# Where matmul operands start: ring tiles 64 bytes longer, 512-column operands level with the large buffers, values operands 64 bytes above

## The chip, the core and the metric

The kernel runs on one core of a Trainium2 chip. The metric is the device time of one execution in microseconds; lower is better. Before the change it is 1809.54 us, the median of 3 runs (1808.73 to 1810.48).

## What is computed

Two inputs, a prompt and a sample, each of 512 tokens by 1024, pass through the same two layers in fp32: one of differential attention, one of bidirectional retention. The reference, cut to what matters:

```python
def trunk(x, ...):
    for i in range(2):
        h = rms_norm(x, norm_g[i], 1e-6)
        x = x + (diff_attention(h, ...) if i == 0 else bidir_retention(h, ...))
    return rms_norm(x, final_norm_g, 1e-6)

def diff_attention(h, w_in, ...):
    q, k, v, gate = split(h @ w_in)            # 1024 -> 4 * 2048, 8 heads
    p = softmax(q @ k.T)                       # two score maps a head, rotary q and k
    a = p[:, :, 0] - lam * p[:, :, 1]
    o = rms_norm(a @ v, subln_g) * silu(gate)
    return o @ w_out                           # 2048 -> 1024
```

`bidir_retention` has the same frame (projection, gate, output projection); its scores are masked by a decay instead of a softmax, forward and backward, and carry a state from one half of the sequence to the other.

## The kernel before

**Three passes for a product.** An fp32 operand is split into a high part of reduced precision (fp32r) and the rest. A product takes three matmuls (`PASSES`, line 32): high by high, high by low, low by high. The high part is cast by ScalarE (`hi_of`, line 399, recorded at line 400), the rest is a subtraction on VectorE (`lo_of`, line 402, recorded at line 403).

**Projections.** The input projections are made in 2 by 2 blocks with seven products P1 to P7 for eight (`SEQ`, line 43). `make_b` (line 448) makes the seven transposed activation operands B11 to T4, each of four tiles of 128 by 2 by 512, in 28 large buffers ("slots"). A `Unit` (line 518) is 512 columns of weights. `prep` (line 551) puts a weight operand in a tile of the ring `ws` (7 tiles of 4096 bytes a partition), and `product` (line 586) multiplies:
- a "pair" unit (q, k and gate) streams the large buffer, 512 columns, past weights from the ring: line 599;
- a "wide" unit (values) streams the ring tile, 256 columns, past weights from the large buffer: line 609.

**Attention and retention.** Scores of the first layer stream k past q, 512 columns (line 1116); the product of the score map with the values is at line 1181, 256 columns. Its transposes are at line 1161. In the second layer, lines 1315 (scores), 1339 (state), 1359 and 1367 (output) all have 256 columns. The output projection of either layer streams a ring tile of `out_weights` (line 862), 512 columns, past the head's output oT (line 891).

**Where buffers lie.** 18 of the large buffers are cuts of one tile, the arena, 4096 bytes apart (`slot`, line 303); the others (numbers 12, 13 and from 20 on) are tiles of the pool `cp`. A cut may be shifted by some elements of 4 bytes: k of the first layer by 16, v by 16, oT by 32 (`new_oT`, line 826), and so on. A shifted cut reaches into the next one's start, so each has a second name, its edge, by which the planner sees such neighbours. The arena begins with 32 unused elements and is 80 longer than its 18 cuts. Small columns (row maxima, sums, scales, a few elements each) have a pool `sm` of their own, which lies first; the ring is in the pool `wk` with the other work tiles, behind the arena.

**Who sets the order.** Every operation is recorded with a cost, what it reads and what it writes. `Plan.arrange` (line 138) simulates the engines with these costs and writes an order for each engine by hand; matmuls keep the recorded order within a window of 24. The order therefore depends on the names by which operations are tied, edges among them, and not on addresses. Loads go through SyncE's queue.

Of the kernel before, what the change touches and what calls it, by code (L numbers as in the profile page):

```python
# [9 lines left out]
F32 = mybir.dt.float32  # L10
F32R = mybir.dt.float32r
# [4 lines left out]
P = 128  # L16
S = 512
D = 1024
KT = D // P
NT = S // P  # L20
NH = 8
# [11 lines left out]
WS_BUFS = 7  # L33
# [220 lines left out]
def trunk_kernel(  # L254
# [9 lines left out]
    ys = (y_prompt, y_sample)  # L264
    plan = Plan()

    sm = ctx.enter_context(tc.tile_pool(name="sm", bufs=1))
    cp = ctx.enter_context(tc.tile_pool(name="cp", bufs=1))
    ar = ctx.enter_context(tc.tile_pool(name="ar", bufs=1))
    wk = ctx.enter_context(tc.tile_pool(name="wk", bufs=1))  # L270
# [2 lines left out]
    dr = ctx.enter_context(tc.tile_pool(name="dr", bufs=1, space=bass.MemoryType.DRAM))  # L273


    SIZE = dict(ws=1024, raw=1024, st=1024, c=512, e=512, m=512, os=1024)
    places = {}
    cnt = [0]

    def view(pool, tag, i, size, shape, dt=F32):  # L280


        if size % 16 and pool in (cp, wk):
            pool = sm
        if (tag, i) not in places:
            places[tag, i] = pool.tile([P, size], F32, tag=f"{tag}{i}", name=f"{tag}_{i}", bufs=1)
        n = math.prod(shape[1:])
        t = places[tag, i][0:shape[0], 0:n]
        if dt != F32:
            t = t.bitcast(dt)  # L290
        if len(shape) == 3:
            t = t.rearrange("p (a b) -> p a b", a=shape[1])
        elif len(shape) == 4:
            t = t.rearrange("p (a b c) -> p a b c", a=shape[1], b=shape[2])
        return t

    def work(tag, shape, bufs, dt=F32, name=None):
        size = SIZE.get(tag, shape[1])
        return Buf(plan, tag, bufs, lambda i: view(wk, tag, i, size, shape, dt))

    arena = ar.tile([P, 18 * 1024 + 80], F32R, tag="arena", name="arena")

    def slot(n, shape, dt=F32R, shift=0):

        size = math.prod(shape[1:])
        at = None if n in (12, 13) or n >= 20 else n if n < 12 else n - 2
        if at is None:
            assert not shift  # L310
            cnt[0] += 1
            label = f"b_{cnt[0]}"
            return Buf(plan, f"b{n}", 1, lambda i: cp.tile(shape, dt, tag=f"b{n}", name=label))
        assert dt == F32R
        lo = 32 + at * 1024 + shift

        def make(i):
            t = arena[:, lo:lo + size]
            return t.rearrange("p (a b) -> p a b", a=shape[1]) if len(shape) == 3 else t
        b = Buf(plan, f"b{n}", 1, make)  # L320
        b.also = Buf(plan, f"edge{at + 1 if shift else at}", 1, None)
        return b

    def const(shape, tag, dt=F32, size=None):
        return Buf(plan, tag, 1, lambda i: view(cp, tag, i, size or math.prod(shape[1:]), shape, dt))

    def ws_t(shape):
        return work("ws", shape, WS_BUFS, F32R)

    def raw_t(shape):  # L330
        return work("raw", shape, 4)
# [1 line left out]
    def st_t(shape, name="st"):  # L333
        return work("st", shape, 3, name=name)
# [18 lines left out]
    def bank(tag, name=None):  # L353
        return Buf(plan, tag, BUFS[tag], lambda i: view(pj if tag == "pj" else sc, tag, i, S, [P, S]))
# [16 lines left out]
    def dve(n, fn, r, w, wait=0.0):  # L371
        plan.op("DVE", 0.07 + 0.00104 * n, fn, r, w, wait=wait)
# [20 lines left out]
    def dma(out, in_, r, w, kb, eng=None):  # L393

        q = eng or nc.sync
        plan.op("SP" if eng is None else "ACT", 0.62, lambda: q.dma_start(out(), in_()), r, w, lands=2.0 + kb / 200.0,
                kb=kb, load=any(isinstance(k[0] if isinstance(k, tuple) else k, Buf) for k in w))

    def hi_of(n, dst, src, r, w):
        act(n, lambda: nc.scalar.copy(dst(), src()), r, w)  # L400

    def lo_of(n, dst, src, hi, r, w):
        dve(n, lambda: nc.vector.tensor_tensor(dst(), src(), hi().bitcast(F32), op=ALU.subtract), r, w)  # L403
# [39 lines left out]


    Bop = {}
    powers = const([P, NH, NT], "powers", size=64)

    def make_b(layer, source):


        def parts(name, k, hi, lo, r):
            t = slot(B_SLOT[name] + k, [P, 2, S])
            hi(lambda: t[:, 0, :], r, [(t, 0)])
            lo(lambda: t[:, 1, :], lambda: t[:, 0, :], r + [(t, 0)], [(t, 1)])
            Bop[name, k] = t
# [62 lines left out]
    class Unit:  # L518
# [32 lines left out]
        def prep(self, op):  # L551
            x = self.take
            n = 256 if self.wide else P

            def combine(a, b, fn):
                t = st_t([P, 4, n])
                out = ((lambda: self.like(t.t)), t)
                dve(4 * n, lambda: nc.vector.tensor_tensor(out[0](), a[0](), b[0](), op=fn), [a[1], b[1]], [t])
                return out
            if op == "P1":  # L560
                src = x(0, 0)
            elif op == "P2":
                src = x(0, 1)
            elif op == "P4":
                src = x(1, 1)
            elif op == "P5":
                src = self.s[1] = combine(x(1, 0), x(1, 1), ALU.add)
            elif op == "P6":
                src = self.s[2] = combine(self.s[1], x(0, 0), ALU.subtract)
            elif op == "P3":  # L570
                src = combine(x(0, 1), self.s[2], ALU.subtract)
            else:
                src = combine(x(0, 0), x(1, 0), ALU.subtract)
            if self.wide:
                a, b = ws_t([P, 4, n]), ws_t([P, 4, n])
                hi, lo = ((lambda: a.t), a), ((lambda: b.t), b)
            else:
                s = ws_t([P, 2, 4, n])
                hi, lo = ((lambda: s[:, 0]), (s, 0)), ((lambda: s[:, 1]), (s, 1))
            hi_of(4 * n, lambda: self.like(hi[0]()), src[0], [src[1]], [hi[1]])  # L580
            lo_of(4 * n, lambda: self.like(lo[0]()), src[0], lambda: self.like(hi[0]()), [src[1], hi[1]], [lo[1]])
            self.ops[op] = (hi, lo)
            if op == "P2" and self.early is not None:
                self.early, self.x = None, {}
# [239 lines left out]
        return rr  # L824

    def new_oT(g):
        return [slot(16 + 2 * g + a, [P, 2, S], F32R, 32) for a in range(2)]

    def load_qk(src, i, shift):
        t = slot(i, [P, 2, S], F32R, shift)  # L830
        dma(lambda: t.t.bitcast(F32), lambda: src[0][src[1]], [src[0]], [t], 512)
        return t
# [95 lines left out]
    qk_d = {}  # L928
# [164 lines left out]
    qk, vt, sg, oT = {}, {}, {}, {}  # L1093
    st = [{} for _ in tiles]

    def fetch1(h, g, v=True):
        for j in range(2):
            for which in range(2):
                qk[h, g, j, which] = load_qk((qk_d[0, which, h, g], j), 6 * which + 2 * g + j, 16 * which)
        if v:  # L1100
            fetch1_v(h, g)

    def fetch1_v(h, g):
        vt[h, g] = load_v(v_d[0, h, g], 10 + 4 * g, 16)
        sg[h, g] = load_sg(g_d[0, h, g])
# [108 lines left out]
    def at(f, i, n):  # L1214
        if 0 <= i < n:
            f(i)

    fetch1(0, 0)
    fetch1(0, 1, False)
    turns2 = itertools.chain(["sc", "o", "sc", "o"], itertools.cycle(["tp", "o"]))  # L1220
    made = make_b(1, x_source(1, xN, lambda g: next(turns2) if g else "pj"))

    for i in range(N + 5):
        if i % 2 and i > 2:
            fill(1, LAG)
            at(av, i - 3, N)
        at(scores, i, N)
        at(row_max, i, N)
        at(exps, i, N)
        at(combine, i, N)  # L1230
        for n, when in enumerate((0, 1, 2, 3)):
            if i == when:
                step(proj, 1)
                if n >= 2:
                    new_xN(n - 2, lambda t, n=n: (xs[n - 2][0, t * P:(t + 1) * P, :], []))
                if n == 3:
                    fetch1_v(0, 1)
        if not i % 2 or i < 3:
            fill(1, LAG)
        at(transp, i - 1, N)  # L1240
        fill(1, LAG)
        if i % 2 == 0 and i > 3:
            at(weighed, i - 4, N)
        if i < N and i % 4 == 2 and i > 4:
            nh, ng = tiles[i][0:2]
            if ng == 1 and nh + 1 < NH:
                fetch1(nh + 1, 0)
            elif ng == 0 and nh > 0:
                fetch1(nh, 1)
# [20 lines left out]
    qk, vt, sg, oT = {}, {}, {}, {}  # L1270
# [78 lines left out]
    def av2(b, c):  # L1349
# [29 lines left out]
        if c == 0:  # L1379
            settle(h - 1, g)  # L1380
            oT[h, g] = new_oT(g)
# [71 lines left out]
    for i in range(N2 + 1):  # L1453
        if i < N2:
            b, c = chunks[i]
# [8 lines left out]
            if i == N2 - 1:  # L1464
                for n in range(2):
                    f = fin_ps[n] = bank("sc", "fin")
# [67 lines left out]
```

## Time and profile before

| | |
|---|---|
| median of 3 runs | 1809.54 us |
| span of the profiled execution | 1807.0 us |
| TensorE busy | 1794.9 us, 10299 matmuls |
| weight loads (PEld) | 1558.1 us |
| VectorE, ScalarE, GpSimd busy | 1477.1, 895.1, 169.5 us |
| mean granted TensorE clock | 0.999 |
| DMA | 328.81 MB, 182 GB/s on average |

The span runs from the first to the last instruction of one profiled execution, and its sums are compared with that span; the runs' time is some 2.5 us above it. In lines of the timeline, the first two numbers are the start in us and the duration of a merged row of like instructions; a matmul's end is modelled and overlaps the next one's start, so the pace is the distance from one row's start to the next row's. In grouped lines, the pair behind the bar is busy time in us and mean ns of one instruction, followed by the engine's idle time before them. In the chain, the pair is the start and the duration of a piece.

### The profile page before, as it was taken

The numbers are of one execution on the slowest core, as the hardware profiler recorded it, in microseconds if no ns is written. First come the engines' busy times: TensorE is split into PE (matmuls) and PEld (weight loads), VectorE is DVE, ScalarE is ACT, GpSimd is POOL, SyncE is SP. The second block draws the span as 40 slices with busy tenths as digits, with TensorE's granted clock in tenths as the row PEclk, the third lists the DMA queues.
The fourth block names the chain that finished last, engine by engine and source line by source line (L and its number), as shares of the span: only waits on it lengthen the run. The fifth ranks groups of instructions, "written<-read, shape, count | busy, mean of one in ns | idle before, by whom it ended". The sixth has DMA issues, their size and how long they took to land.

```text
span 1807.0 us, 27780 instructions
## 1 busy us (share of the span) xinstructions
PE 1794.9 (99%) x10299; PEld 1558.1 (86%) x10299; DVE 1477.1 (82%) x2319; ACT 895.1 (50%) x1856; POOL 169.5 (9%) x323
## 2 busy tenths in 40 slices
PE   9999999999999999999999999999999999999998
PEld 6789889898988888888888888898989898888887
DVE  7958787778699888888888897787887967888887
ACT  7753444433434565554555866444434355444346
POOL 1000000000000022222322300000000000111113
PEclk9999999999999999999999999999999999999999
DMA  6444455555545685444554524464657559765662
GB/s 217 134 126 137 161 140 178 184 168 155 174 126 175 201 334 198 178 156 159 190 204 140 190 73 146 140 210 146 205 156 228 151 170 396 272 238 182 225 218 94
DMA packets 162767, 328.81 MB, mean 182 GB/s; under 512 B 12724, under 2 KB 76872, under 8 KB 162632
## 3 DMA queue, kind: packets, MB, share of 16 engines
q1 hardware_dynamic: 162304, 326.71, 54.1%
q8 instruction: 81, 1.33, 0.3%
q14 instruction: 54, 0.44, 0.1%
q10 hardware_dynamic: 328, 0.34, 0.1%
HBM read 209.55 MB, written 117.44 MB: 181 GB/s over the span
## 4 chain that ended last, share of the span: by engine, by line
PE 93%; DVE 2%; DMA 2%; ACT 2%; issue 1%; POOL 0%; SPq 0%; POOLq 0%; DVEq 0%; ACTq 0%
PE pj L599 20%; PE pj L891 19%; PE sc L599 10%; PE pj L609 10%; PE o L599 8%; PE o L1181 5%; PE sc L1116 5%; PE sc L609 5%; PE o L609 2%; PE o L1359 2%; PE tp L1161 2%; PE sc L1315 1%; PE o L1367 1%; PE tp L1339 1%; DMA raw<-in_ret_w_out_dram 1%
## 5 line engine op out<-in xcount | busy, mean ns | idle before, releaser
L891 PE MATMUL pj<-ws,arena 128*128 128x512 f32 x1542 | 391.2, 397 | 0.0
L891 PEld LDWEIGHTS pj<-ws,arena 128*128 128x128 f32 x1542 | 277.7, 188 | 52.7
L599 PE MATMUL pj<-b,ws 128*128 128x512 f32 x1080 | 265.0, 392 | 0.0
L599 PEld LDWEIGHTS pj<-b,ws 128*128 128x128 f32 x1080 | 201.4, 188 | 43.0
L403 DVE TENSOR_TENSOR ws<-st,ws 128x512 fp32r<-128x512 f32 (+1 forms) x192 | 147.9, 774 | 74.8 <-ACT ws L400 56.7
L896 DVE SCALAR_TENSOR_TENSOR b<-pj,crr,b 128x512 f32<-128x512 f32 (+1 forms) x257 | 189.9, 744 | 21.4 <-PE pj L891 21.0
L403 DVE TENSOR_TENSOR ws<-raw,ws 128x512 fp32r<-128x512 f32 (+1 forms) x164 | 141.5, 868 | 71.3 <-ACT ws L400 61.0
L400 ACT CAST ws<-st 128x512 fp32r<-128x512 f32 (+1 forms) x192 | 132.4, 693 | 121.4 <-PE pj L599 36.4
L599 PE MATMUL sc<-arena,ws 128*128 128x512 f32 x768 | 186.8, 392 | 0.0
L599 PE MATMUL o<-arena,ws 128*128 128x512 f32 x744 | 180.0, 393 | 1.1 <-ACT m L385 0.6
L599 PEld LDWEIGHTS sc<-arena,ws 128*128 128x128 f32 x768 | 144.0, 188 | 31.3
L400 ACT CAST ws<-raw 128x512 fp32r<-128x512 f32 (+1 forms) x164 | 125.7, 772 | 87.0 <-PE o L599 45.0
L599 PEld LDWEIGHTS o<-arena,ws 128*128 128x128 f32 x744 | 138.4, 188 | 31.7 <-DVE arena L463 1.4
L599 PE MATMUL pj<-arena,ws 128*128 128x512 f32 x648 | 160.3, 392 | 0.4 <-DVE arena L463 0.4
L599 PEld LDWEIGHTS pj<-arena,ws 128*128 128x128 f32 x648 | 120.8, 188 | 26.7 <-DVE arena L463 0.7
L1134 ACT ACTIVATE b<-sc,nm 128x512 f32<-128x512 f32 x128 | 88.0, 689 | 66.9 <-DVE nm L1124 66.5
L636 ACT COPY c<-pj 128x512 f32<-128x512 f32 x104 | 60.9, 586 | 119.7 <-PE pj L599 66.4
L609 PE MATMUL pj<-ws,b 128*128 128x256 f32 x960 | 116.8, 276 | 0.0
L609 PEld LDWEIGHTS pj<-ws,b 128*128 128x128 f32 x960 | 113.2, 188 | 0.7
L1116 PE MATMUL sc<-arena 128*128 128x512 f32 x384 | 101.2, 395 | 0.3 <-ACT b L1134 0.3
L1181 PEld LDWEIGHTS o<-arena 128*128 128x128 f32 x768 | 93.1, 188 | 2.7
L1181 PE MATMUL o<-arena 128*128 128x256 f32 x768 | 93.7, 278 | 0.0
(207 smaller groups left out, 2855.9 us busy)
## 6 DMA issues: line engine op xcount, KB each, us to landing
qk<-os SPq DMA_DIRECT2D x192, 256.0 KB, 3.6
arena<-qk SPq DMA_DIRECT2D x96, 512.0 KB, 5.8
raw<-in_da_w_in_dram SPq DMA_DIRECT2D x64, 512.0 KB, 5.1
v<-os SPq DMA_DIRECT2D x64, 512.0 KB, 4.3
arena<-v SPq DMA_DIRECT2D x64, 512.0 KB, 4.1
raw<-in_ret_w_in_dram SPq DMA_DIRECT2D x48, 512.0 KB, 4.8
os<-g SPq DMA_DIRECT2D x32, 512.0 KB, 7.4
g<-e SPq DMA_DIRECT2D x48, 256.0 KB, 4.6
```

Source lines behind the costliest of these rows:

```text
L400: act(n, lambda: nc.scalar.copy(dst(), src()), r, w)
L403: dve(n, lambda: nc.vector.tensor_tensor(dst(), src(), hi().bitcast(F32), op=ALU.subtract), r, w)
L599: nc.tensor.matmul(ps.t, a[u][0]()[:, k, :], bt[k][:, v, :], start=(opens and k == 0 and i == 0), stop=(k == 3 and i == 2), skip_group_che ...
L609: nc.tensor.matmul(ps[:, (t % 2) * 256:(t % 2) * 256 + 256], bt[k][:, v, t * P:(t + 1) * P], a[u][0]()[:, k, :], start=(opens and t % 2 == ...
L636: act(S, lambda c=c, ps=ps: nc.scalar.copy(c.t, ps.t), [ps], [c])
L891: nc.tensor.matmul(ps[:, here], o[a][:, e, t * P:(t + 1) * P], u[b][:, e, here], start=(m == 0), stop=(m == 5))
L896: axpy(n, lambda half=half, here=here, ps=ps: nc.vector.scalar_tensor_tensor(half, ps[:, here], rr[:, t % 2:t % 2 + 1], half, op0=ALU.mult ...
L1116: nc.tensor.matmul(s.t, q[:, a, t * P:(t + 1) * P], k[:, b, :], start=(n == 0), stop=(n == 2))
L1134: act(840, lambda j=j, s=s, m=m: nc.scalar.activation(p[:, j, :], s.t, AF.Exp, bias=m.t, accum_out=sm[:, 2 * j + n:2 * j + n + 1]), [s, m] ...
L1161: nc.tensor.transpose(tp[:, j * P:(j + 1) * P], p[:, 0, j * P:(j + 1) * P], ident.t)
L1181: nc.tensor.matmul(o[:, e * 256:(e + 1) * 256], v[b][:, j, e * P:(e + 1) * P], aT[a][:, j, :], start=(n == 0), stop=(n % 12 == 11), skip_g ...
L1359: nc.tensor.matmul(o[:, e * 256:(e + 1) * 256], v_[v][:, 2 * c + j, e * P:(e + 1) * P], a_[:, u, j * 256:(j + 1) * 256], start=(e == 0 and ...
```

## The change

The pool of small columns goes. Each of the 7 ring tiles becomes 1024 + 16 elements, a tile of its own in the arena's pool, directly behind the arena. Between two ring tiles lies a pad of 48 elements, and columns of up to 32 elements are cut from these pads one after another. A ring tile is used from its start by 512-column matmuls (pair units, output projection), and from element 16 on, 64 bytes above, by values products (`wide`). The arena loses its 32 leading elements; k of the first layer loses its shift; oT's shift grows from 32 to 64 elements.

With this, the large buffers in `cp`, the arena's unshifted cuts and the ring tiles all start at the same place modulo 256 bytes, and oT too, whose shift is 256 bytes.

```diff
-    sm = ctx.enter_context(tc.tile_pool(name="sm", bufs=1))
...
     def view(pool, tag, i, size, shape, dt=F32):
-        if size % 16 and pool in (cp, wk):
-            pool = sm
+        n = math.prod(shape[1:])
         if (tag, i) not in places:
-            places[tag, i] = pool.tile([P, size], F32, tag=f"{tag}{i}", name=f"{tag}_{i}", bufs=1)
-        n = math.prod(shape[1:])
+            if size <= 32 and pool in (cp, wk):
+                k = next(k for k, used in enumerate(gaps) if used + size <= PAD - 16)
+                places[tag, i] = pads[k][:, gaps[k]:gaps[k] + size]
+                gaps[k] += size
+            else:
+                places[tag, i] = pool.tile([P, size], F32, tag=f"{tag}{i}", name=f"{tag}_{i}", bufs=1)
...
-    arena = ar.tile([P, 18 * 1024 + 80], F32R, tag="arena", name="arena")
+    PAD = 64
+    gaps = [0] * (WS_BUFS - 1)
+    arena = ar.tile([P, 18 * 1024 + 64], F32R, tag="arena", name="arena")
+    rings, pads = [], []
+    for i in range(WS_BUFS):
+        rings.append(ar.tile([P, 1024 + 16], F32R, tag=f"ws{i}", name=f"ws_{i}"))
+        if i < WS_BUFS - 1:
+            pads.append(ar.tile([P, PAD - 16], F32, tag=f"pad{i}", name=f"pad_{i}"))
...
-        lo = 32 + at * 1024 + shift
+        lo = at * 1024 + shift
...
-    def ws_t(shape):
-        return work("ws", shape, WS_BUFS, F32R)
+    def ws_t(shape, wide=False):
+        def make(i):
+            lo = 16 if wide else 0
+            t = rings[i][:, lo:lo + 1024]
+            if len(shape) == 3:
+                return t.rearrange("p (a b) -> p a b", a=shape[1])
+            return t.rearrange("p (a b c) -> p a b c", a=shape[1], b=shape[2])
+        return Buf(plan, "ws", WS_BUFS, make)
...
-    powers = const([P, NH, NT], "powers", size=64)
+    powers = const([P, NH, NT], "powers")
...
-                a, b = ws_t([P, 4, n]), ws_t([P, 4, n])
+                a, b = ws_t([P, 4, n], True), ws_t([P, 4, n], True)
...
-        return [slot(16 + 2 * g + a, [P, 2, S], F32R, 32) for a in range(2)]
+        return [slot(16 + 2 * g + a, [P, 2, S], F32R, 64) for a in range(2)]
...
-                qk[h, g, j, which] = load_qk((qk_d[0, which, h, g], j), 6 * which + 2 * g + j, 16 * which)
+                qk[h, g, j, which] = load_qk((qk_d[0, which, h, g], j), 6 * which + 2 * g + j, 0)
```

More of the change, by code (lines that the diff above doesn't have):

```diff
@@ L273, in trunk_kernel @@
     dr = ctx.enter_context(tc.tile_pool(name="dr", bufs=1, space=bass.MemoryType.DRAM))
-    SIZE = dict(ws=1024, raw=1024, st=1024, c=512, e=512, m=512, os=1024)
+    SIZE = dict(raw=1024, st=1024, c=512, e=512, m=512, os=1024)
     places = {}
```

## The prediction

> **What bounds the kernel now.** I read the core's span and clock first, then the busy line of the page, then the chain of waits, then PE's waits.
>
> ```profile
> core 0: 1807.0 us, clock 0.999
> PE 1794.9 (99%) x10299; PEld 1558.1 (86%) x10299; DVE 1477.1 (82%) x2319; ACT 895.1 (50%) x1856; POOL 169.5 (9%) x323
> PE 93%; DVE 2%; DMA 2%; ACT 2%; issue 1%; POOL 0%; SPq 0%; POOLq 0%; DVEq 0%; ACTq 0%
> PE sc L1010 <- DVE minus L411: 1.4, 1, 1.4
> PE tp L1028 <- DVE arena L463: 1.0, 2, 0.7
> ```
>
> TensorE has work for 1794.9 of 1807.0 us at a clock of 0.999, the chain is 93% PE, and the two longest of PE's waits are 1.4 and 1.0 us in total. So the end is set by how fast matmuls follow each other. The "mean ns of one" of a matmul (about 392) overlaps its neighbours; the pace has to be read from starts. The longest pieces of the chain are the cleanest place, since the same instruction repeats there without a wait:
>
> ```profile
> 75.27 8.24 PE pj L599 x36
> 1783.58 13.76 PE pj L891 x60
> ```
>
> 36 matmuls of 512 columns in 8.24 us are 228.9 ns each; 60 of the output projection in 13.76 us are 229.3. The pace of 256 columns comes from the timeline, as the distance between the starts of two rows:
>
> ```profile
> 303.18 5.60 PE L609 MATMUL sc<-ws,arena 128*128 128x256 f32 x48
> 308.62 0.84 PE L609 MATMUL pj<-ws,b 128*128 128x256 f32 x6
> ```
>
> 308.62 - 303.18 = 5.44 us over 48 is 113.3 ns. Two of them take 226.7: a 512-column matmul costs 2.2 ns more than its two halves would. Remember this number; it is the term that the forecast uses.
>
> **What the change moves.** No operation is added or removed; every engine has as many instructions as before. What moves is where operands lie. From the placement in the built programs, each operand's start modulo 256 bytes, moving minus stationary:
> - L599 (moving: large buffer; stationary: ring tile), L891 (ring; oT) and L1116 (k; q): +64 before, 0 after.
> - L609 (moving: ring tile; stationary: large buffer): -64 before, +64 after.
> - L1181, L1339, L1315 (-64) and L1359, L1367 (+64): unchanged.
> Also, large buffers and rings began 32 bytes beyond a multiple of 64; now they begin on a multiple of 64.
>
> How many matmuls this touches:
>
> ```profile
> L891 PE MATMUL pj<-ws,arena 128*128 128x512 f32 x1530 | 389.8, 398 | 0.0
> L599 PE MATMUL pj<-b,ws 128*128 128x512 f32 x1080 | 265.0, 392 | 0.0
> L599 PE MATMUL sc<-arena,ws 128*128 128x512 f32 x768 | 186.8, 392 | 0.0
> L599 PE MATMUL o<-arena,ws 128*128 128x512 f32 x744 | 180.0, 393 | 1.1 <-ACT m L385 0.6 <-DVE arena L463 0.3
> L599 PE MATMUL pj<-arena,ws 128*128 128x512 f32 x648 | 160.3, 392 | 0.4 <-DVE arena L463 0.4
> L599 PE MATMUL sc<-b,ws 128*128 128x512 f32 x120 | 29.1, 391 | 0.0
> L1116 PE MATMUL sc<-arena 128*128 128x512 f32 x384 | 101.2, 395 | 0.3 <-ACT b L1134 0.3
> L609 PE MATMUL pj<-ws,b 128*128 128x256 f32 x960 | 116.8, 276 | 0.0
> L609 PE MATMUL sc<-ws,arena 128*128 128x256 f32 x768 | 89.6, 276 | 0.0
> L609 PE MATMUL pj<-ws,arena 128*128 128x256 f32 x576 | 73.1, 277 | 0.0
> L609 PE MATMUL o<-ws,arena 128*128 128x256 f32 x384 | 45.0, 277 | 0.0
> ```
>
> 512 columns: 1530 + 3360 (the five L599 rows) + 384 = 5274. Values products: 960 + 768 + 576 + 384 = 2688.
>
> **(1) 512 columns, +64 to 0.** No steady run of the profile has level operands, so the price is bounded by the nearest rows. First, does an offset matter at all? One stretch of the second layer holds runs at both offsets:
>
> ```profile
> 1603.61 0.86 PE L1339 MATMUL tp<-arena 128*128 128x256 f32 x6
> 1604.31 0.87 PE L1315 MATMUL sc<-arena 128*128 128x256 f32 x6
> 1605.01 1.54 PE L891 MATMUL pj<-ws,arena 128*128 128x512 f32 x6
> 1606.39 1.52 PE L1359 MATMUL o<-arena 128*128 128x256 f32 x12
> 1607.75 0.84 PE L1367 MATMUL o<-arena,b 128*128 128x256 f32 x6
> 1608.43 1.55 PE L891 MATMUL pj<-ws,arena 128*128 128x512 f32 x6
> ```
>
> Distances of starts: L1359 (+64) 1.36/12 = 113.3 and L1367 (+64) 0.68/6 = 113.3, but L1339 and L1315 (-64) 0.70/6 = 116.7. The six L891 take 1.38 us; five at 228.9 leave 235.5 for the sixth, during which the weights of L1359 are read, 64 bytes above the ring tile that streams. So about 3.4 ns per 256 columns and 6.6 per 512 can hang on where operands lie. But -64 isn't always dear: L609 (-64) runs at 113.3. Two places show a level weight read once, at the end of a run:
>
> ```profile
> 1303.79 2.91 PE L599 MATMUL pj<-arena,ws 128*128 128x512 f32 x12
> 1306.54 5.63 PE L609 MATMUL pj<-ws,b 128*128 128x256 f32 x48
> 926.12 2.90 PE L1181 MATMUL o<-arena 128*128 128x256 f32 x24
> 928.86 1.54 PE L1116 MATMUL sc<-arena 128*128 128x512 f32 x6
> ```
>
> The twelfth L599 streams a large buffer while L609's weights, from another large buffer, are read: both start 32 bytes past a multiple of 256. Twelve take 2.75 us, 229.2 each: a single level read costs nothing that shows. L1181's last one is level with L1116's weights too: 24 take 2.74 us, 114.2 each, near the pace of 113.3.
> Bounds per 512-column matmul, then: dearest +6.6 ns (the sixth L891): 5274 x 6.6 = +34.8 us. Cheapest, without another mechanism: as fast as its two halves, 228.9 - 226.7 = -2.2 ns: -11.6 us. I take -2.2. The surplus of 2.2 over two halves exists only at 512 columns, the level read seen once isn't dear, and operand offset is the one thing that differs for it; the rows at -64 are an offset that the 512s never have, before or after. The choice is an inference; the trace has no steady level run that proves it.
>
> **(2) Values products, -64 to +64.** 113.3 before (L609) and 113.3 for the rows that already have +64 (L1359, L1367): 0. If they fell to the pace of L1315 instead, 2688 x 3.4 = +9.1 us.
>
> **(3) Small columns between the ring tiles.** Their writers and readers keep their order in kind; they are ACT, DVE and POOL work that is hidden behind PE: ACT has half of the span free, POOL 91%, and DVE 18%. Waits stay nearly as many in the built program (PE: 1114 on other engines' semaphores and DMAs before, 1109 after), so sharing a tile adds no chain of false waits: 0. If DVE's free 330 us (1807.0 - 1477.1) were eaten, DVE would be the bound; that needs each of its 2319 instructions to grow by 142 ns.
>
> **(4) Order.** q and k tiles without a shift touch other neighbours in the arena, and the planner's order changes in one place: PE's order is the same up to matmul 3394 and differs for some 250 of the next 300, where attention begins. That is inside this window:
>
> ```profile
> 620.00:690.00 70.00, 69.69 (x387) 59.04 (x387) 54.95 (x92) 42.45 (x103) 12.45 (x30) 1.00 0.88 325
> ```
>
> Columns after the stretch are PE, PEld, DVE, ACT and POOL busy, clock, DMA share, GB/s. PE idles 0.3 of 70 us, with the DMA at 0.88. Moving a few products by one place can win at most 0.3 us, and lose about what PE's two longest waits above cost, 1 to 2 us, if a product comes ahead of its load. I take 0, bounds -0.3 and +2.
>
> **Sum.** -11.6 + 0 + 0 + 0: 1807.0 - 11.6 = 1795.4 us for the profiled execution. The median of the runs is 1809.5, 2.5 above that span, so 1797.9 on the metric.
>
> **Rivals.**
> - *Level weight reads disturb the stream* (slower). In a long level run every weight load, not one, meets the moving reads, and each matmul pays what L1315 pays over L1359, 3.4 ns, up to the 6.6 of the sixth L891. For it: those rows. Against: the two level places above. 5274 x 3.4 = +17.9 us: 1827.4; at 6.6, 1844.3. It decides as soon as 36 chained L599 take longer than 8.24 us, and shows on the whole kernel from +0.7 ns each.
> - *Offsets don't matter for 512 columns* (the change does nothing to time). For it: 229.2 with a level read against 228.9 without; L609 at -64 as fast as L1359 at +64. Then 1809.5.
>  The Trainium skill, SBUF — State Buffer, section "SBUF: two separate sides", has PE on ports of its own that never wait on anyone, and TensorE: Matmul & The Clock Gate, section "Part 2: What happens when you issue a matmul", gives it two independent read ports, one for the moving operand and one for LDWEIGHTS. By that rule this rival is right. L609 agrees with it (113.3 at -64); L1315's 116.7 against L1359's 113.3, same size, doesn't.
> - *The start on a multiple of 64 is what helps* (much faster). A 512-column operand that begins 32 bytes off a multiple of 64 touches 33 pieces of 64 bytes, an aligned one 32. If each piece costs the same, a matmul saves 228.9/33 = 6.9 ns: 5274 x 6.9 = 36.4 us, 1773.1; with the 2688 values products saving 113.3/17 = 6.7 as well, another 18 us: 1755. For it: 113.3 is 17 times 6.67. Against: 228.9 isn't 33 times 6.67 (220), and nothing in this trace starts aligned.
>  The Trainium skill, TensorE: Matmul & The Clock Gate, section "Back-to-back issue gap", has 512 columns at N/2.4 + 2.5 = 215.8 ns; an estimate by it would be 5274 x 13.1 = 69 us off. No run here shows that pace.
>
> **How the numbers follow.** About 0.2% (3.6 us) is what a measurement of this kernel can tell from no change. Forecast, -2.2 ns per 512 columns: 0.42. Aligned starts, or another gain that is larger: 0.13. Nothing: 0.12. Level reads disturb: 0.28. The rest slower (values products at L1315's pace, or the shared tile of small columns delaying DVE): 0.05. Faster is thus 0.55, same 0.12, slower 0.33. The range goes from the 512-column saving of aligned starts (1773, taken as 1772) to between the slower rival's two prices (1827 and 1844), 1838. The forecast's own range, if its mechanism holds, is 1793 to 1806.
>
> **What would show it.** Right: chain pieces of 36 L599 at about 8.16 us (36 x 226.7) and L891 alike, L609 still 48 in 5.44, span near 1795. Wrong, slower: L599 pieces over 8.24 with L609 unchanged. Aligned starts: 36 L599 near 7.99 us, and L609 at 48 in 5.12; L1359 and L1367, whose offset isn't changed, also faster, which only this rival expects. Nothing: all pieces as quoted. If (2) is wrong, L609 alone moves; if (3), PE shows new waits for DVE, ACT or POOL; if (4), idle of PE in 620 to 690.

## The result and the profile after

The change makes the kernel slower: 1817.93 us, the median of 5 runs (1817.51 to 1818.54), against 1809.54 (5 runs, 1808.50 to 1810.48). The ratio is 1.0044, with a 95% interval of 1.0032 to 1.0057. The profiled execution has a span of 1815.6 us, 8.6 above that of before. Line numbers have moved by 17: L616 is what was L599, L626 was L609, L908 was L891, L1133 was L1116, L1198 was L1181, and L1332, L1356, L1376 and L1384 were L1315, L1339, L1359 and L1367. Below, the lines are called by the work that they do, with the number of before.

Three lines of the page of after, the span, the busy line and the chain's shares, answer to those of before:

```profile
core 0: 1815.6 us, clock 0.999
PE 1801.2 (99%) x10299; PEld 1572.6 (87%) x10299; DVE 1477.2 (81%) x2319; ACT 895.1 (49%) x1856; POOL 171.6 (9%) x323
PE 92%; DMA 3%; DVE 2%; ACT 1%; issue 0%; SPq 0%; POOL 0%; POOLq 0%; DVEq 0%; ACTq 0%
```

The clock is the same, VectorE, ScalarE and GpSimd are within 2.1 us of their old sums, and PE still carries the chain. PE's busy time grew by 6.3 us and its idle time by 2.3 (1815.6 - 1801.2 = 14.4 us against 12.1). So the loss is mostly in the pace of matmuls. From the chain of after, start and duration of two of its longest pieces:

```profile
1149.55 8.16 PE pj L616 x36
1792.27 13.66 PE pj L908 x60
```

These are faster: 36 in 8.16 us are 226.7 ns each instead of 228.9, just what was forecast, and the output projection's 60 take 227.7 instead of 229.3. The values products, from the timeline of after:

```profile
303.06 5.81 PE L626 MATMUL sc<-ws,arena 128*128 128x256 f32 x48
308.71 0.87 PE L626 MATMUL pj<-ws,b 128*128 128x256 f32 x6
```

48 of them take 308.71 - 303.06 = 5.65 us instead of 5.44: 117.7 ns each instead of 113.3. The second layer's stretch, again from the timeline of after:

```profile
1610.97 0.88 PE L1356 MATMUL tp<-arena 128*128 128x256 f32 x6
1611.68 0.85 PE L1332 MATMUL sc<-arena 128*128 128x256 f32 x6
1612.37 1.55 PE L908 MATMUL pj<-ws,arena 128*128 128x512 f32 x6
1613.76 1.58 PE L1376 MATMUL o<-arena 128*128 128x256 f32 x12
1615.17 0.87 PE L1384 MATMUL o<-arena,b 128*128 128x256 f32 x6
1615.88 1.55 PE L908 MATMUL pj<-ws,arena 128*128 128x512 f32 x6
```

L1376's twelve now take 1.41 us, where the same twelve took 1.36; L1384's six take 0.71 instead of 0.68. Neither line's operands were moved against each other by the change. And the six of the output projection take 1.39 us, as long as before (1.38). Over the whole trace its 129 runs of six gained nothing (237.7 ns each on average, 237.6 before), while its 53 runs of twelve went from 234.5 to 231.9 ns each and the long run at the end gained too.

With all starts of each trace added up, line by line (from each start to the next, in us):

| line of before | before | after | difference |
|---|---|---|---|
| L599, projections, 512 | 774.3 | 768.5 | -5.8 |
| L891, output projection, 512 | 360.8 | 359.1 | -1.7 |
| L1116, scores, 512 | 89.8 | 90.5 | +0.7 |
| L609, values products, 256 | 305.7 | 317.1 | +11.4 |
| L1181, map by values, 256 | 88.4 | 90.0 | +1.6 |
| L1359 and L1367, output of layer two, 256 | 65.9 | 68.3 | +2.4 |
| L1315 and L1339, 256 | 45.1 | 45.1 | 0 |

These rows make +8.6 us, the difference of the spans; smaller rows, which are left out, cancel to within 0.4. The 512s gain 6.8 us, the 256s lose 15.4. The +0.7 of L1116 is no slower pace: its row holds one wait, for ScalarE's work at L1134 (L1151 in the kernel after), in which two starts lie 1.35 us apart.

### The profile page after: what moved, and what is told of

The parts are those of the page before. It is cut to its first block, busy times and chain, and to the rows that moved or that the text cites. A ratio compares the mean times of both kernels' runs of the same rounds, so it can differ in the third digit from the quotient of the medians.

```text
span 1815.6 us, 27774 instructions
## 1 busy us (share of the span) xinstructions
PE 1801.2 (99%) x10299; PEld 1572.6 (87%) x10299; DVE 1477.2 (81%) x2319; ACT 895.1 (49%) x1856; POOL 171.6 (9%) x323
## 4 chain that ended last, share of the span: by engine, by line
PE 92%; DMA 3%; DVE 2%; ACT 1%; issue 0%; SPq 0%; POOL 0%; POOLq 0%; DVEq 0%; ACTq 0%
PE pj L616 20%; PE pj L908 19%; PE sc L616 10%; PE pj L626 10%; PE o L616 8%; PE sc L626 5%; PE o L1198 5%; PE sc L1133 4%; PE o L626 2%; PE o L1376 2%; PE tp L1178 1%; PE o L1384 1%; PE tp L1356 1%; PE sc L1332 1%; DMA raw<-in_ret_w_out_dram 1%; DVE ws L420 1%
## 5 line engine op out<-in xcount | busy, mean ns | idle before, releaser
L908 PE MATMUL pj<-ws,arena 128*128 128x512 f32 x1542 | 389.6, 396 | 0.0
L908 PEld LDWEIGHTS pj<-ws,arena 128*128 128x128 f32 x1542 | 277.6, 188 | 50.7
L616 PE MATMUL pj<-b,ws 128*128 128x512 f32 x1080 | 263.1, 391 | 0.2 <-DVE e L661 0.2
L616 PEld LDWEIGHTS pj<-b,ws 128*128 128x128 f32 x1080 | 201.4, 188 | 41.7 <-DVE e L661 0.6
L913 DVE SCALAR_TENSOR_TENSOR b<-pj,pad,b 128x512 f32<-128x512 f32 (+1 forms) x257 | 190.5, 745 | 22.0 <-PE pj L908 21.2
L616 PE MATMUL sc<-arena,ws 128*128 128x512 f32 x768 | 185.2, 390 | 0.0
L616 PE MATMUL o<-arena,ws 128*128 128x512 f32 x744 | 178.8, 391 | 1.1 <-ACT m L402 0.6
L616 PEld LDWEIGHTS sc<-arena,ws 128*128 128x128 f32 x768 | 144.0, 188 | 29.8
L616 PEld LDWEIGHTS o<-arena,ws 128*128 128x128 f32 x744 | 138.4, 188 | 30.6 <-DVE arena L480 1.4
L616 PE MATMUL pj<-arena,ws 128*128 128x512 f32 x648 | 159.2, 391 | 0.3 <-DVE arena L480 0.3
L616 PEld LDWEIGHTS pj<-arena,ws 128*128 128x128 f32 x648 | 120.9, 188 | 25.6 <-DVE arena L480 0.6
L1151 ACT ACTIVATE b<-sc,pad 128x512 f32<-128x512 f32 x128 | 87.9, 688 | 69.8 <-DVE pad L1141 68.9
L626 PE MATMUL pj<-ws,b 128*128 128x256 f32 x960 | 120.8, 280 | 0.0
L626 PEld LDWEIGHTS pj<-ws,b 128*128 128x128 f32 x960 | 117.0, 188 | 0.6
L1133 PE MATMUL sc<-arena 128*128 128x512 f32 x384 | 99.9, 394 | 0.9 <-ACT b L1151 0.9
L1198 PEld LDWEIGHTS o<-arena 128*128 128x128 f32 x768 | 94.4, 189 | 3.2 <-ACT arena L417 0.7
L1198 PE MATMUL o<-arena 128*128 128x256 f32 x768 | 95.2, 281 | 0.5 <-ACT arena L417 0.5
```

Of the source, the lines that this page charges most:

```text
L616: nc.tensor.matmul(ps.t, a[u][0]()[:, k, :], bt[k][:, v, :], start=(opens and k == 0 and i == 0), stop=(k == 3 and i == 2), skip_group_che ...
L626: nc.tensor.matmul(ps[:, (t % 2) * 256:(t % 2) * 256 + 256], bt[k][:, v, t * P:(t + 1) * P], a[u][0]()[:, k, :], start=(opens and t % 2 == ...
L908: nc.tensor.matmul(ps[:, here], o[a][:, e, t * P:(t + 1) * P], u[b][:, e, here], start=(m == 0), stop=(m == 5))
L913: axpy(n, lambda half=half, here=here, ps=ps: nc.vector.scalar_tensor_tensor(half, ps[:, here], rr[:, t % 2:t % 2 + 1], half, op0=ALU.mult ...
L1133: nc.tensor.matmul(s.t, q[:, a, t * P:(t + 1) * P], k[:, b, :], start=(n == 0), stop=(n == 2))
L1151: act(840, lambda j=j, s=s, m=m: nc.scalar.activation(p[:, j, :], s.t, AF.Exp, bias=m.t, accum_out=sm[:, 2 * j + n:2 * j + n + 1]), [s, m] ...
```

## The experiments

Two questions: is it the new offset of the values products that costs (their own +64 bytes), or something that follows from the level 512s; and what of the 512s' gain holds alone. Offsets are, as in the prediction, moving operand minus stationary operand, modulo 256 bytes. The table gives the pace of each kind in ns, from start to start inside the runs of a line, over the whole trace of each kernel, and the ratio to the kernel before on the same chip. Where runs are short (L891, L1181, L1359), such a mean moves by up to half a ns with the distances that are left out of it. Matmuls come in the order of before in e3, e5, e6 and e13, and in the order of the change in the others; the two orders differ only where attention begins.

| kernel | median us | ratio, 95% | L599 | L891 | L609 | L1181 | L1359 |
|---|---|---|---|---|---|---|---|
| before | 1809.54 | | 228.9 | 229.4 | 113.3 | 114.6 | 113.8 |
| after | 1817.93 | 1.0044, 1.0032 to 1.0057 | 226.9 | 227.5 | 117.8 | 116.9 | 117.5 |
| e1, values at 0 | 1823.44 | 1.0075, 1.0060 to 1.0090 | 226.8 | 228.8 | 120.0 | 117.0 | 117.4 |
| e2, all 32 bytes on | 1817.51 | 1.0044, 1.0029 to 1.0059 | 226.9 | 228.8 | 117.8 | 116.8 | 117.4 |
| e3, before, starts on 64 | 1809.79 | 1.0001, 0.9992 to 1.0011 | 228.9 | 229.4 | 113.4 | 114.6 | 113.3 |
| e4, values at -64 | 1816.67 | 1.0041, 1.0026 to 1.0055 | 226.8 | 227.9 | 117.5 | 117.7 | 117.4 |
| e5, old offsets, new layout | 1809.03 | 1.0003, 0.9994 to 1.0013 | 228.9 | 229.3 | 113.4 | 115.6 | 113.3 |
| e6, only L599 level | 1813.28 | 1.0027, 1.0016 to 1.0038 | 226.8 | 229.2 | 117.5 | 115.4 | 113.4 |
| e7, only L891 and L1116 level | 1811.61 | 1.0019, 1.0009 to 1.0028 | 228.9 | 227.9 | 113.4 | 117.7 | 117.4 |
| e8, values at +32 | 1813.37 | 1.0028, 1.0016 to 1.0040 | 226.8 | 227.4 | 116.7 | 117.0 | 117.4 |
| e13, only values at +64 | 1821.99 | 1.0072, 1.0058 to 1.0085 | 228.9 | 229.3 | 117.8 | 115.6 | 113.9 |

### First round: which offset costs

**e1: values products level too**, the change with

```diff
-            lo = 16 if wide else 0
+            lo = 0
```

> The changed kernel with the values operands level too (0 instead of +64). Its profile showed 512-column matmuls at 226.8 ns (228.9 before) but values products at 117.8 (113.3 before). Theory 'start' (the place of an operand relative to a multiple of 64 bytes sets the pace of 256 columns: 113.3 at 32 past, 117.8 on it): L609 stays at 117.8, about 1818 us. Theory 'offset' (moving minus stationary sets it; +64 is worse than -64): L609 leaves 117.8, either way. Theory 'rhythm' (256 columns keep the rhythm in which the 512-column runs leave the array, and level runs leave a worse one): 117.8, 1818.

Measured: 1823.44 us. In its timeline, where the change has 5.65:

```profile
303.80 5.92 PE L626 MATMUL sc<-ws,arena 128*128 128x256 f32 x48
309.56 0.88 PE L626 MATMUL pj<-ws,b 128*128 128x256 f32 x6
```

48 in 5.76 us: 120.0 ns. Level is the worst of the places tried for values products, and the best one found for 512 columns. So an offset isn't good or bad as such.

**e2: the change, 32 bytes on**, so that all large operands start 32 bytes beyond a multiple of 64, as before the change, with the offsets between them kept:

```diff
+    lead = cp.tile([P, 8], F32, tag="lead", name="lead")
```

> The changed kernel with one unused tile of 32 bytes in front, so that every large buffer and ring tile starts 32 bytes past a multiple of 64, as before the change; all offsets between operands stay those of the change. Theory 'start': L609 back to 113.3 (2688 x 4.4 ns = 11.9 us off) and L1181, L1359, L1367 back too (some 3 us), 512 columns stay at 226.8: 1802 to 1806 us. Theories 'offset' and 'rhythm': as the changed kernel, 1818.

Measured: 1817.51 us, and L599 and the values products at the pace of the change; only L891 is some 1 ns slower than there, as it is in e1, with the same offsets. **e3: the kernel before, on a multiple of 64**, its old offsets kept:

```diff
-    gcol = const([P, 28], "gcol")
+    gcol = const([P, 24], "gcol")
```

> The kernel before with one column tile 16 bytes shorter, which moves all large buffers and ring tiles 32 bytes down, onto multiples of 64; offsets between operands stay those of before. Theory 'start': L609 at 117.8 and the other 256-column lines up too, 512 columns unchanged at 228.9: about 1822 to 1825 us. Theories 'offset' and 'rhythm': as before, 1809.5.

Measured: 1809.79 us, a ratio of 1.0001. Where operands start in absolute terms, on a multiple of 64 or 32 beyond it, does nothing to the time that can be measured in either kernel. What counts is how far apart the two operands of a matmul are.

**e4: 512s level, values products back at -64**, by a ring that begins 64 bytes lower:

```diff
-    arena = ar.tile([P, 18 * 1024 + 64], F32R, tag="arena", name="arena")
+    arena = ar.tile([P, 18 * 1024 + 112], F32R, tag="arena", name="arena")
...
-            lo = 16 if wide else 0
+            lo = 0 if wide else 16
```

> The changed kernel with ring tiles 64 bytes lower relative to the large buffers and the two uses swapped: 512 columns from element 16 (level, as in the change), values products from element 0 (-64, as before the change). Theory 'offset': L609 back to 113.3, about 1806 us. Theories 'start' and 'rhythm': L609 at 117.8, 1818.

Measured: 1816.67 us; values products at 117.5 ns although their offset is the old one, at which the kernel before has 113.3. Undoing the edit that the loss sits on doesn't undo the loss. Something else in the change slows them too.

### Second round: one part at a time

**e5: the new layout with all old offsets** (the pool of small columns gone, columns in the pads, the ring behind the arena):

```diff
-    arena = ar.tile([P, 18 * 1024 + 64], F32R, tag="arena", name="arena")
+    arena = ar.tile([P, 18 * 1024 + 112], F32R, tag="arena", name="arena")
...
-                a, b = ws_t([P, 4, n], True), ws_t([P, 4, n], True)
+                a, b = ws_t([P, 4, n]), ws_t([P, 4, n])
...
-        return [slot(16 + 2 * g + a, [P, 2, S], F32R, 64) for a in range(2)]
+        return [slot(16 + 2 * g + a, [P, 2, S], F32R, 32) for a in range(2)]
...
-                qk[h, g, j, which] = load_qk((qk_d[0, which, h, g], j), 6 * which + 2 * g + j, 0)
+                qk[h, g, j, which] = load_qk((qk_d[0, which, h, g], j), 6 * which + 2 * g + j, 16 * which)
```

> Control: pads, packed columns, ring stride and order of the change, but every offset between operands as before it (512 columns +64, values -64, k shifted by 16, oT by 32). If the offsets alone carry the loss (theories 'offset' and 'rhythm'): L599 at 228.9, L609 at 113.3, L1359 at 113.7, about 1809.5 us. If packed columns, the ring's stride or the order carry it: L609 stays near 117.5 and the time near 1817.

Measured: 1809.03 us, 1.0003. The layout and the shared pads cost nothing that can be measured (L1181, whose offset is the same, is slower by 0.8 us in sum, of which more at the end). This kernel is the base of those that follow. From its timeline:

```profile
302.96 5.60 PE L626 MATMUL sc<-ws,arena 128*128 128x256 f32 x48
308.40 0.84 PE L626 MATMUL pj<-ws,b 128*128 128x256 f32 x6
```

**e6: of e5, only the pair units' ring tiles level**, so that L599 alone goes from +64 to 0:

```diff
-                s = ws_t([P, 2, 4, n])
+                s = ws_t([P, 2, 4, n], True)
```

> As the control, with L599 alone level. Theory 'rhythm' (256-column runs are slow because the 512-column runs ahead of them are level): L599 226.8, L609 117.5 though its own offset is that of before, L1359 and L1367 (which follow L891, not level here) back at 113.7; about 1814 us (-6 for L599, +11 for L609). Theory 'own offset': L609 stays at 113.3, about 1803.5 us.

Measured: 1813.28 us, 4.2 above e5. A piece of its chain, and its timeline at the same place as above:

```profile
1148.33 8.16 PE pj L616 x36
```

```profile
302.91 5.82 PE L626 MATMUL sc<-ws,arena 128*128 128x256 f32 x48
308.56 0.87 PE L626 MATMUL pj<-ws,b 128*128 128x256 f32 x6
```

The level 512s hold their gain alone: 8.16 us for 36. But the values products, whose operands are those of e5, take 5.65 us for 48 instead of 5.44. Summed by line: L599 768.0 us against 774.3 in e5 (-6.3), L609 316.2 against 305.9 (+10.3). That makes +4.0 of the 4.2. Run by run it is sharper. In e4 and e6 each run of values products behind a run of L599 has 117.8 (all 8 runs of 240 matmuls, 11 of 48 and 4 of 12); the five runs that come behind transposes have 113.3 to 113.4.

**e7: of e5, only output projection and scores level** (L891 and L1116; L599 and L609 as before):

```diff
-        hi, lo = ws_t([P, 2, S]), ws_t([P, 2, S])
+        hi, lo = ws_t([P, 2, S], True), ws_t([P, 2, S], True)
```

with the shifts of oT and k as in the change.

> As the control, with L891 and L1116 level and L599 not. Theory 'rhythm': L599 228.9 and L609 113.3 as before, L891 near 227.5, L1359, L1367 and L1181 (which follow level runs) at 117; about 1811 us. Theory 'own offset': L1359 and L1367 stay at 113.7, about 1808 us.

Measured: 1811.61 us. Two stretches of the second layer, e5 and then e7, from their timelines:

```profile
1606.76 1.52 PE L1376 MATMUL o<-arena 128*128 128x256 f32 x12
1608.12 0.84 PE L1384 MATMUL o<-arena,b 128*128 128x256 f32 x6
1608.80 1.56 PE L908 MATMUL pj<-ws,arena 128*128 128x512 f32 x6
```

```profile
1607.38 1.58 PE L1376 MATMUL o<-arena 128*128 128x256 f32 x12
1608.80 0.87 PE L1384 MATMUL o<-arena,b 128*128 128x256 f32 x6
1609.50 1.55 PE L908 MATMUL pj<-ws,arena 128*128 128x512 f32 x6
```

L1376 and L1384 have the same offsets in both, and go from 1.36 and 0.68 us to 1.42 and 0.70. Over the whole trace, L1359 goes from 113.3 to 117.4, L1367 from 113.4 to 117.3 and L1181 from 115.6 to 117.7, while L609, which has no level 512s ahead of it here, stays at 113.4. This is e6's finding at other lines: 256s slow down where the 512s next to them were made level. (e7's order of matmuls is that of the change and e5's that of before, but at L1359 and L1367 both have the same.)

**e8: the change, values products at +32:**

```diff
-            lo = 16 if wide else 0
+            lo = 8 if wide else 0
```

> The changed kernel with values operands 32 bytes above the level instead of 64. Theory 'rhythm': L609 stays at about 117.8 or rises towards the 120.0 that it had at 0; 1818 to 1823 us. Theory 'own offset': an offset exists at which L609 falls to 113.3; if this is it, 1806 us.

Measured: 1813.37 us, 4.6 below the change; values products at 116.7 ns. The 1.1 ns less make 3.0 us over 2688. +32 is the better of the two offsets, and still loses more than the 512s gain.

### Third round: does the run ahead decide?

If values products keep the pace in which the run ahead leaves them, one other instruction between should bring 113.3 back. **e9: e6 with one 128-column transpose of `ident` ahead of the first values product of P1 and of P2** (it replaces the four that the first unit has; its result is overwritten by the product that opens the bank; apart from transposes, the matmuls of e9, e10, e14 and e16 come in the order of before):

```diff
-                if self.led and op == "P1" and t == 0:
-                    for j in range(NT):
+                if op in ("P1", "P2") and t == 0:
+                    for j in range(1):
                         nc.tensor.transpose(ps[:, j * P:(j + 1) * P], ident.t, ident.t)
```

> Projections level and the rest as in the control, as in the run with only the projections level (L609 117.5 after L599, but 113 in the five runs that follow transposes); now one 128-column transpose of the identity stands ahead of the P1 and P2 products of every values unit (16 in all, some 0.11 us each; 2304 of the 2688 values matmuls lie behind one; the first unit had four there already). Theory 'rhythm' (the step of one other matmul is enough to let 256 columns fall into the fast rhythm): L609 behind a transpose at 113.3, L599 at 226.8; 1813.3 - 2304 x 4.17 ns + 16 x 0.11 us = about 1805.5 us, below the kernel before. Rival (the five runs were fast for another reason): L609 stays at 117.5, about 1815 us.

Measured: 1807.66 us, ratio 0.9992 (0.9982 to 1.0003). Its timeline:

```profile
294.22 2.89 PE L616 MATMUL pj<-b,ws 128*128 128x512 f32 x12
296.95 0.27 PE L623 MATMUL o<-ident 128*128 128x128 f32 x1
296.98 5.70 PE L626 MATMUL o<-ws,arena 128*128 128x256 f32 x48
302.51 5.60 PE L626 MATMUL sc<-ws,arena 128*128 128x256 f32 x48
307.95 0.84 PE L626 MATMUL pj<-ws,b 128*128 128x256 f32 x6
```

After the level L616 and one transpose (L623), 48 values products take 5.44 us again, and all 8 runs of 240 have 113.3. L609 comes to 309.0 us instead of e6's 316.2. Without the transpose, in e6, the same 8 runs have 117.8. Not all runs are cured: three of the four P1 runs of 48 keep 117.8 behind their transpose, and the 8 runs of P4, which have none ahead, keep it too. The times of e9's 11 executions fall into two groups, 1806.5 to 1807.7 (six) and 1810.4 to 1811.2 (five); one trace can't tell which runs differ between them.

**e10: two transposes instead of one** (`range(2)`):

> The same with two transposes. If any interruption by another kind of matmul resets the rhythm, as with one: L609 at 113.3, about 1807 us. If it is a step that counts, so that one and two differ (three L599 took 687 ns before the change, a rhythm of three): one of the two runs has 113.3 and the other 117.5.

Measured: 1815.89 us, 1.0032 (1.0021 to 1.0043); L609 at 116.3 on average. Of the 8 runs of 240 three have 113.3 and five 117.8. More distance isn't safer; a second transpose puts most runs back at the slow pace.

**e11: of e6, L599 at +32 instead of 0** (`lo = 8 if wide else 0`), and **e12: at +128**, with the values products at -64 and the output projection at +64 in both. e12's edit, on e5:

```diff
-    arena = ar.tile([P, 18 * 1024 + 112], F32R, tag="arena", name="arena")
+    arena = ar.tile([P, 18 * 1024 + 96], F32R, tag="arena", name="arena")
...
-                a, b = ws_t([P, 4, n]), ws_t([P, 4, n])
+                a, b = ws_t([P, 4, n], True), ws_t([P, 4, n], True)
...
-        hi, lo = ws_t([P, 2, S]), ws_t([P, 2, S])
+        hi, lo = ws_t([P, 2, S], True), ws_t([P, 2, S], True)
```

> Projections with moving minus stationary at +32 (level is 0, before was +64), the rest as in the control. If level alone gives 226.8: L599 at or above 228.9 and L609 near 113.3, about 1809. If every offset below 64 has the rhythm of level: L599 226.8, L609 117.5, about 1813.

> Projections at +128. If the place modulo 128 is what counts, this is level again: L599 226.8, L609 117.5, about 1813. If modulo 256 counts, something else: 228.9 or more for L599.

Measured: 1833.39 us (1.0129, 1.0115 to 1.0143) and 1827.18 us (1.0096, 1.0081 to 1.0111). A piece of e11's chain, then one of e12's:

```profile
76.05 8.40 PE pj L616 x36
```

```profile
75.83 8.36 PE pj L616 x36
```

36 of L599 take 8.40 us at +32 and 8.36 at +128, against 8.24 at +64 and 8.16 at 0; from starts inside the long runs it is 233.3, 232.4, 228.9 and 226.8. +128 and +64 would be the same place as 0 if only the place within 64 bytes counted; they aren't. Behind these runs too, the values products at -64 are slow, though no longer all of them: in e11 all 23 runs behind L599, in e12 7 of the 8 runs of 240 but only 1 of the 11 of 48. So level isn't special for what comes behind: of the four offsets tried for L599, +64, that of before, is the only one behind which every run of values products at -64 keeps 113.3.

### Fourth round: the values products' own offset, and a cure

**e13: of e5, only the values products moved, to +64:**

```diff
-        rings.append(ar.tile([P, 1024 + 16], F32R, tag=f"ws{i}", name=f"ws_{i}"))
+        rings.append(ar.tile([P, 1024 + 32], F32R, tag=f"ws{i}", name=f"ws_{i}"))
...
-            lo = 16 if wide else 0
+            lo = 32 if wide else 0
```

with the values tiles taken `True` and pads of 32 elements.

> As the control (every offset as before the change), with the values operands alone at +64 instead of -64. Theory 'rhythm': L599 228.9 and L609 113.3 with the own offset costing nothing, about 1809 us. Rival (the own offset costs too): L609 above 114, at 117.8 about 1821.

Measured: 1821.99 us, 13.0 above e5. Its chain and its timeline:

```profile
75.64 8.24 PE pj L616 x36
```

```profile
305.38 5.82 PE L626 MATMUL sc<-ws,arena 128*128 128x256 f32 x48
311.03 0.87 PE L626 MATMUL pj<-ws,b 128*128 128x256 f32 x6
```

With the 512s as before (8.24 us), the new offset of the values products alone makes them 117.7 and L609's sum 317.0 us instead of 305.9, +11.1 of the 13. So two causes are each enough for the slow pace of L609: its own +64, and level 512s ahead (e6).

**e14: e6 with the transpose ahead of P2 alone, e16: e9 with one ahead of P4 as well.** For e14 the condition becomes `(self.led and op == "P1" or op == "P2") and t == 0`.

> Only the projections level, one transpose ahead of the P2 product of each values unit (8 runs of 240 matmuls) and ahead of the first unit's P1. Theory 'rhythm': the runs of 240 at 113.3, P1 runs of 48 behind level L599 at 118; L599 226.8; 0.5 us below e9 or level with it, about 1807 us where the kernel before has 1809. If the order of the other work is the larger part of e9's time: within 1 us of e9 either way.

> As e9, with one more transpose of the identity, into the spare bank tp, ahead of the P4 product of each values unit (8 runs of 48 matmuls that stood at 118 in e9). Theory 'rhythm': those fall to 113.3: 8 x 48 x 4.4 ns - 8 x 0.11 us = 0.8 us below e9, about 1807 us where the kernel before has 1809. Rival (a transpose starts the fast rhythm only behind some moments of the level run): part of the runs stay at 118 and the time stays at e9's or above.

Measured: 1808.46 us (0.9994, 0.9985 to 1.0003) and 1808.49 us (0.9996, 0.9987 to 1.0005). In e14 6 of the 8 runs of 240 have 113.3; in e16 6 of 8, and of 12 runs of 48 behind a transpose 6 have 113 and 6 have 118. More transposes don't cure more runs.

**e15: the change itself, with e9's transposes**, values products at +64.

> The changed kernel (512 columns level, values at +64) with one transpose ahead of the P1 and P2 products of each values unit. Theory 'rhythm' as so far told, for any values offset: the runs of 240 fall to 113.3, about 1817.9 - 8 = 1810 us. If at +64 the slow rhythm is the only one that lasts once level runs are ahead: L609 stays at 117.8, about 1820 us.

Measured: 1820.23 us, 1.0062 (1.0048 to 1.0075). Its timeline behind a transpose:

```profile
297.58 0.27 PE L623 MATMUL o<-ident 128*128 128x128 f32 x1
297.61 5.90 PE L626 MATMUL o<-ws,arena 128*128 128x256 f32 x48
...
303.35 5.81 PE L626 MATMUL sc<-ws,arena 128*128 128x256 f32 x48
309.00 0.87 PE L626 MATMUL pj<-ws,b 128*128 128x256 f32 x6
```

48 still take 5.65 us, and every run of this trace has 117.8. What cures the old offset doesn't cure the new one. In the change, then, undoing either cause alone doesn't help, which is why e4 fell flat.

No version beats the kernel before clear of the noise: the intervals of e9, e14 and e16 all hold 1.

## Why the prediction was wrong

It forecast 1797.9 us and faster; it is 1817.93 and slower. That lies inside its range of 1772 to 1838, but on the side that it thought less likely. Of the reason it had one half, values products at a slower pace, among the rest that it gave 0.05; the other half, level 512s that slow down the 256s behind them, none of its rivals had.

**(1) 512 columns, +64 to 0: right in mechanism, too large in size.** The term was -2.2 ns for each of 5274, -11.6 us. L599 does run at 226.8 when level, on its own (e6) as in the change. But the term was worked out from the chain's longest pieces and applied to every matmul, while the gain belongs to long runs: it measured -5.8 us for L599 (2.2 x 3360 would be 7.4), whose 30 runs of twelve gained nothing (median 229.8 ns each, 229.0 before), -1.7 for L891, whose runs of six gained nothing either, and +0.7 for L1116, which has runs of three and six only. Together -6.8. L1116's runs of six keep their pace (median 230.2 ns each, 229.5 before); what its row adds is the wait, 0.9 us of idle time ahead of it against 0.3, and belongs to (4):

```profile
L1133 PE MATMUL sc<-arena 128*128 128x512 f32 x384 | 99.9, 394 | 0.9 <-ACT b L1151 0.9
```

**(2) Values products, -64 to +64: the step that failed.** "113.3 before (L609) and 113.3 for the rows that already have +64 (L1359, L1367): 0." The first half of the failure is the carry-over: L1359's pace at +64 was read between other neighbours and lent to L609. e13, which makes this move alone, has 117.8 ns and +11.1 us. The prediction's own bound for the step, 3.4 ns and +9.1 us, was the nearer value, though still too low. The second half is that the step was taken for the only one that concerns 256 columns. L1359, L1367 and L1181, noted as "unchanged", lost 4.0 us together, and 3.0 of it comes already in e7 against e5, with level 512s next to them and their own offsets unchanged. e6 shows that the values products would have lost 10.3 us at their old offset too. The prediction's test "if (2) is wrong, L609 alone moves" was wrong with it. The profile before already had a sign: the row means of L1339 and L1315, 116.7 each, were read as the price of -64, but the distances between single starts differ. In the stretch that the prediction shows, L1339 has 122, 116, 114, 113, 114, 117 ns and L1315 114, 119, 117, 118, 118, 118 ns, at the same offset: the one row is on its way to the fast pace, the other stays at the slow one.

**(3) Small columns between the ring tiles, 0: right.** e5 has them, with all old offsets, at 1.0003 (0.9994 to 1.0013).

**(4) Order, 0, bounds -0.3 and +2: a loss within the bound.** The same window of after:

```profile
620.00:690.00 70.00, 68.33 (x379) 58.02 (x378) 53.21 (x90) 40.38 (x98) 12.37 (x27) 1.00 0.86 314
```

PE is busy 68.33 of 70 us instead of 69.69: 1.4 us idle more, over half of the 2.3 by which PE's idle time grew in the whole span. e4 and e7 have the same shifts of k and oT, and so the new order, with other offsets; in the same window PE is busy in e4, e7 and e5 for

```profile
620.00:690.00 70.00, 69.27 (x386) 58.90 (x385) 54.31 (x91) 41.75 (x102) 12.37 (x27) 1.00 0.86 314
```

```profile
620.00:690.00 70.00, 69.26 (x385) 58.72 (x384) 53.77 (x90) 41.41 (x102) 12.91 (x28) 1.00 0.86 312
```

```profile
620.00:690.00 70.00, 69.69 (x387) 59.01 (x387) 54.89 (x91) 42.37 (x102) 12.58 (x30) 1.00 0.87 325
```

The new order leaves 0.4 us more idle there in two of these three traces with it and 1.4 in the third, the change, where the wait of L1116 comes on top; the old order (e5) leaves what before left. A small loss, then, which no run has by itself.

**The rivals.** "Level weight reads disturb the stream" had the right sign and the wrong place: what it said would slow down, the level 512s, got faster, and the decision it named (36 of L599 above 8.24 us) fell against it. For 256 columns level was the slowest place: 120.0 at 0 (e1), behind level 512s. "Offsets don't matter for 512 columns" fell: 226.8, 228.9, 233.3 and 232.4 at 0, +64, +32 and +128. The rule of the Trainium skill that stood behind it (SBUF — State Buffer, "SBUF: two separate sides": PE's ports wait on no one) doesn't cover this: e13 moves one operand by 128 bytes, with the same instructions, and costs 13 us; the measurement decides. "The start on a multiple of 64 is what helps" fell with e2 and e3.

## What to carry to other kernels

The relative place of moving and stationary operand was worth up to 3% of a matmul here at 512 columns (226.8 to 233.3 ns) and 6% at 256 (113.3 to 120.0). Where a kernel is bound by the pace of back-to-back matmuls, it has to be measured for the shape and the neighbours that will really run: a pace read at one line, or in long runs, isn't a price for another line. When a change speeds up one kind of run, look at the paces of the unchanged kinds behind it, line by line, before calling the change good. An edit that undoes a suspected cause and changes nothing (e4) hasn't cleared the cause; do it alone as well (e13), since two causes may each be enough.

## What the runs showed of the hardware

- **At one and the same offset, 256 columns have two paces, 113.3 and 117.8 ns, and whole runs of up to 240 keep one of them.** At -64, in one trace (e6), runs behind level 512s have 117.8 and runs behind transposes 113.3 to 113.4. That what stands ahead bears on the pace is shown by e6, e7 and e9. It doesn't settle it alone: the kernel before has both paces too, unnoticed. Of L1181's 22 runs behind L891, all at the same offsets, 13 are near 113 and 9 near 118; in e5, with these offsets unchanged, 16 are near 118; behind level L891 it is 14 of 20 in the change and 20 of 20 in e7. What in TensorE holds the pace isn't shown, and it stays open why one transpose restores the fast pace in all 8 long runs of e9 and two in only 3 (e10), and why short runs behind the same transpose differ.
- **The relative place counts, and not only within 64 or 128 bytes:** 0, +32, +64 and +128 all differ for 512 columns. It counts modulo 256 as far as tried: level pairs of buffers lie many different multiples of 256 bytes apart, and a run of 612 over them keeps 226.7. The order isn't that for 256 columns (values products at 0, +32, +64: 120.0, 116.7, 117.8 ns, behind level 512s).
- **At +64, 512s start 226, 229 and 232 ns apart in a repeating cycle of three** (mean 228.9, in the starts of L599 before); level, they come at an even 226.7, which is two 256s at 113.3.
